# Residual and feed-forward products of 512 columns on split float32r operands

## Chip, cores and metric

One core of a Trainium2 chip runs the whole program. The metric is the device time in microseconds of one execution, as the median of the runs shown; lower is better.

## What is computed

Two hybrid layers (gated delta rule, latent attention and a gated recurrence, mixed by an output matrix) and then two layers of a second block: a feed-forward, a mixer, a second feed-forward. There are 256 tokens of width 1024, all in float32. What the change touches is this part of the reference (shortened):

```python
# hybrid layer, twice
return x + mixed @ w_out                     # mixed: 256 x 2048
...
# second block, l = 0, 1
x = x + 0.5 * swiglu(rms_norm(x, ffn1_norm[l]), ffn1_w_gate[l], ffn1_w_up[l], ffn1_w_down[l])   # width 2816
...
x = x + mixed @ w_out[l]                     # mixed: 256 x 1024
x = x + 0.5 * swiglu(rms_norm(x, ffn2_norm[l]), ffn2_w_gate[l], ffn2_w_up[l], ffn2_w_down[l])
```

## The kernel before, in words

Activations lie features first: a tile is 128 features by 256 tokens, and the residual `x` is eight such tiles. A product in float32 accuracy is made of three float32r products. Every operand is split into a high part and the rest (`split` for activations, `wsplit` for weights): ScalarE casts the high part (`h`, or `wh` for weights), VectorE subtracts it from the operand (`l`, or `wl`). `pair` gives the two parts of an activation as the two halves of one SBUF tile of 128 x 512. Then `mm3` (line 690) issues, per k tile of 128 features,

```python
mm(out, a[0], b[0], start=start, stop=False)   # wh, h
mm(out, a[0], b[1], start=False, stop=False)   # wh, l
mm(out, a[1], b[0], start=False, stop=stop)    # wl, h
```

with the weights stationary (128 x 128) and 256 tokens moving. `unit` (line 708) loops over the k tiles of 128 output features; all products of a unit go into one half of a PSUM bank. There are two rings of four banks, `acc` for such units and `mix` for everything else.

A feed-forward (`ffn`, line 819) has 22 hidden tiles. Per hidden tile a chunk of 1 MB of weights comes from DRAM (`raw`, three slots), gate and up are two units of 8 k tiles into the two halves of one `acc` bank, VectorE multiplies the bank by the norm's factor `rb` in one instruction of 512 columns, ScalarE takes the tanh, VectorE makes (tanh + 1) times gate and times up, and `split` makes the operand of the down product. Down runs over two groups of four output tiles with 22 k tiles each, in pieces of 6, 8 and 8. `feed` (line 808) adds a finished output tile to the residual, and for the next stage makes the split operand (`add_x`) and the sum of squares, which GpSimd accumulates. The output products of the hybrid layers (end of `hybrid`, units of 8 k tiles, twice over the eight tiles) and of the second block's mixers (`out_proj`, line 1587, units of 4 k tiles, twice over the eight tiles) end in `feed` too. In the second pass `feed` also makes the next stage's operand.

`wh` and `wl` have three slots of 128 x 1024 each, so a weight part is made when the unit three before it has ended.

The order of the instructions on each engine is set by a planner (`Order`): the kernel is traced first, each instruction gets a nominal cost (`cost`, line 378), and a list scheduling over the traced dependences writes one fixed order per engine. Each engine then runs its list in order. All instructions are issued at line 543, so rows of the trace are told apart by their tiles: `acc`, `mix`, `wh`, `wl`, `raw`, `x`, and `s` for the work tiles.

Of the kernel before, what the change touches and what calls it, by code (L numbers as in the profile page):

```python
# [13 lines left out]
ALU = mybir.AluOpType  # L14
# [3 lines left out]
P = 128  # L18
# [3 lines left out]
FF = 22  # hidden tiles of a feed-forward  # L22
# tile sizes (columns of 4 bytes) and their slots
SLOTS = {"raw": (2048, 3), "wh": (1024, 3), "wl": (1024, 3), "s1": (256, 20), "s2": (512, 48), "s3": (384, 12),
         "col": (24, 56)}
# order of the 64 rope dimensions: partners lie 16 lanes apart in a quadrant of 32
# [3 lines left out]
# ---------------------------------------------------------------- host layout  # L30
# [3 lines left out]
def _pack(W, chunks):  # L34
    """(first k tile, k tiles, columns) -> flat; each chunk lies [128, k tiles, columns]"""
    out = []
    for k0, kt, cols in chunks:
        w = W[k0 * P:(k0 + kt) * P][:, cols]
        out.append(w.reshape(kt, P, -1).transpose(1, 0, 2).reshape(-1))
    return np.concatenate(out)  # L40
# [46 lines left out]
# order of the 8 tiles of 128 that the second block's output products sum over: four that are ready early, then the rest  # L87
# [27 lines left out]
def gu_pack(G, U):  # L115
    w = np.stack([G.reshape(8, P, FF, P), U.reshape(8, P, FF, P)], axis=3)  # [k, p, j, 2, f]
# [7 lines left out]
# columns of the parameter tile: name -> (offset, columns)  # L124
# [17 lines left out]
def prm_pack(i):  # L142
# [6 lines left out]
    def taps(w):  # [4, C] -> [128, C/128 * 4]  # L149
# [34 lines left out]
# constants that depend on shapes alone  # L184
# [76 lines left out]
# ---------------------------------------------------------------- instruction order  # L261
# The kernel below is traced first; then each engine's instructions are put in an order that keeps the engines busy
# (a list scheduling over the traced dependences with the engines' nominal costs), and issued in that order.
ENG = ("tensor", "scalar", "vector", "gpsimd", "sync")
# how much later than the earliest of its ready instructions an engine may start a more urgent one
SLACK = {"tensor": 0.0, "scalar": 150.0, "vector": 40.0, "gpsimd": 100.0, "sync": 0.0}
PATIENCE = 400  # how far an instruction may fall behind its place in the tracing order
# free slots of a tag below which tiles are given out in tracing order only
RESERVE = {"s1": 6, "s2": 10, "s3": 4, "col": 16, "raw": 3, "wh": 3, "wl": 3, "mix": 2, "acc": 1}
# from the end of an instruction on one engine to the start of a dependent one on another  # L270
# [19 lines left out]
class Tracer:  # L290
    """stands for one engine: notes its instructions instead of issuing them"""
# [8 lines left out]
class Order:  # L300
# [10 lines left out]
    # ---- tracing  # L311
# [42 lines left out]
    def touch(self, op, r, w):  # L354
# [3 lines left out]
        if h is None:  # L358
            h = self.hist[name] = ([], [])  # writes, reads
# [18 lines left out]
    def cost(self, op):  # L378
# [7 lines left out]
        if op.eng == "tensor":  # L386
            rhs = a[2]
            m, n = _free(a[1]), _free(rhs) if fn == "matmul" else a[1].shape[0]
            if rhs.dtype == F32R:
                return max(0.833 * m, (n if n >= 256 else 4 * n) / 2.4) + 2.3, None  # L390
# [38 lines left out]
    # ---- scheduling  # L429
    def schedule(self):  # L430
        """each engine in turn takes, among the instructions that could start within its slack, the first traced; tiles
        get slots in tracing order, or past it while more than the tag's reserve is free"""
# [8 lines left out]
        # urgency: the tracing order for TensorE; for the others, the first TensorE instruction that needs the result  # L441
# [104 lines left out]
# ---------------------------------------------------------------- kernel  # L546
class Kern:
    def __init__(self, ctx, tc, aps):
# [20 lines left out]
        # scratch in DRAM: blocks of the delta rule's triangles, their inverses (zero outside the diagonal blocks)  # L569
# [6 lines left out]
    def start(self):  # L576
        """the first loads in the order of their use, and TensorE kept busy meanwhile, so that its clock is up"""
# [39 lines left out]
    # ---- tiles: few sizes, so that a slot serves every stage  # L617
# [31 lines left out]
    def pair(self):  # L649
        t = self.tile("s2", (P, 2, S), F32R)  # L650
        return t[:, 0, :], t[:, 1, :]
# [18 lines left out]
    # ---- weights: packed chunks streamed from DRAM in order, split exactly into two float32r parts  # L670
# [19 lines left out]
    def mm3(self, out, a, b, start, stop):  # L690
        """a: stationary parts, b: moving parts"""
# [1127 lines left out]
```

## Time and profile before

| | us |
|---|---|
| median of three runs | 1591.09 |
| lowest and highest run | 1589.70, 1593.88 |
| span of the profiled execution, first to last instruction | 1588.5 |
| lowest run less that span (what lies around it) | 1.2 |
| TensorE busy | 1569.5 |
| VectorE busy | 1183.2 |
| ScalarE busy | 836.4 |
| GpSimd busy | 191.8 |

The profile is of one execution. PE is TensorE's product, PEld its load of stationary weights, DVE is VectorE, ACT ScalarE, POOL GpSimd. A product's duration in a row holds the time in which others stream behind it, so cadences are read from the distance of starts. The granted clock is 1.00 at 2.4 GHz and 0.50 at 1.2 GHz.

### The profile page before, as it was taken

To read this page: it belongs to the slowest core of one execution; us is meant where nothing else is said; L and a number is where in the kernel's file an instruction comes from. 1 tells how busy PE (TensorE), PEld (TensorE's weight loads), DVE (VectorE), ACT (ScalarE), POOL (GpSimd) and SP (SyncE) were. 2 spreads that over 40 slices of the span, in tenths; PEclk is the share of its full clock that TensorE was granted. 3 is DMA by queue.
4 is the path that set the end of the run, shared out by engine and by line. 5 is a ranking of instruction groups with operands and counts; after the bars stand their busy time and mean duration, and the time that the engine had idled before them with its cause. 6 is when DMAs were issued, how large, how long until landed. Compare 5 with 4: busy or idle time off the path is not lost.

```text
span 1588.5 us, 31207 instructions
## 1 busy us (share of the span) xinstructions
PE 1569.5 (99%) x12712; PEld 1520.3 (96%) x12712; DVE 1183.2 (74%) x2249; ACT 836.4 (53%) x1508; POOL 191.8 (12%) x196
## 2 busy tenths in 40 slices
PE   8999999999999999999999999999999999999999
PEld 8988999988989999999999999999999998999999
DVE  8987968996987677756888777665777666777753
ACT  5467745547765544445445444555444456654442
POOL 2301002311114100002102000021000321110000
PEclk9999999999999999999999999999999999999999
DMA  8343445343435455454334555544555743355553
GB/s 283 118 140 107 171 140 179 119 143 107 163 133 186 160 186 184 175 185 147 123 117 159 186 186 173 185 176 162 184 186 175 244 145 107 121 173 186 179 173 126
DMA packets 54598, 257.82 MB, mean 162 GB/s; under 512 B 11308, under 2 KB 21688, under 8 KB 27576
## 3 DMA queue, kind: packets, MB, share of 16 engines
q1 hardware_dynamic: 54456, 255.85, 46.9%
q8 instruction: 99, 1.62, 0.4%
q14 instruction: 43, 0.35, 0.1%
HBM read 252.39 MB, written 3.43 MB: 161 GB/s over the span
## 4 chain that ended last, share of the span: by engine, by line
PE 85%; DVE 8%; POOL 2%; issue 2%; ACT 1%; DMA 1%; SPq 0%; POOLq 0%; DVEq 0%; ACTq 0%
PE acc L543 74%; PE mix L543 11%; DVE s L543 5%; DVE wl L543 2%; POOL col L543 1%; POOL s L543 1%; DVE col L543 1%; ACT s L543 1%; ACT wh L543 0%; DMA s<-tri_out 0%; DMA tri_out<-s 0%; DMA prm<-in_prm_dram 0%; SPq L543 0%; DVE x L543 0%; ACT L543 0%
## 5 line engine op out<-in xcount | busy, mean ns | idle before, releaser
L543 PE MATMUL acc<-s,wh 128*128 128x256 f32 x6720 | 1237.5, 285 | 0.0
L543 PEld LDWEIGHTS acc<-s,wh 128*128 128x128 f32 x6720 | 1051.8, 192 | 6.9 <-issue 4.6
L543 PE MATMUL acc<-s,wl 128*128 128x256 f32 x3360 | 957.1, 285 | 1.0 <-DVE wl L543 1.0
L543 ACT ACTIVATE wh<-raw 128x1024 fp32r<-128x1024 f32 (+1 forms) x470 | 489.1, 1041 | 574.9 <-PE acc L543 410.2
L543 DVE TENSOR_TENSOR wl<-raw,wh 128x1024 fp32r<-128x1024 f32 (+1 forms) x470 | 571.4, 1216 | 241.2 <-ACT wh L543 238.8
L543 PEld LDWEIGHTS acc<-s,wl 128*128 128x128 f32 x3360 | 644.9, 192 | 2.4 <-DVE wl L543 1.4
L543 PE MATMUL mix<-s,s 128*128 128x128 f32 (+7 forms) x1072 | 162.4, 291 | 5.7 <-DVE col L543 2.4
L543 POOL TENSOR_TENSOR s<-s,s 128x256 f32<-128x256 f32 x75 | 92.8, 1240 | 597.4 <-ACT s L543 596.2
L543 PEld LDWEIGHTS mix<-s,s 128*128 128x128 f32 (+5 forms) x1072 | 119.0, 168 | 34.8 <-issue 9.1
L543 ACT ACTIVATE s<-s 128x256 fp32r<-128x256 f32 (+3 forms) x311 | 134.1, 439 | 27.0 <-DVE s L543 25.3
L543 DVE TENSOR_TENSOR s<-s,s 128x256 fp32r<-128x256 f32 (+6 forms) x302 | 128.8, 436 | 13.5 <-ACT s L543 8.1
L543 PE MATMUL acc<-wh,s 128*128 128x256 f32 x640 | 126.5, 290 | 0.0
L543 DVE TENSOR_TENSOR s<-acc,s 128x512 f32<-128x512 f32 (+1 forms) x134 | 91.9, 686 | 44.2 <-PE acc L543 43.1
L543 PEld LDWEIGHTS acc<-wh,s 128*128 128x128 f32 x640 | 103.7, 194 | 2.3 <-issue 1.6
L543 PE MATMUL acc<-wl,s 128*128 128x256 f32 x320 | 92.5, 289 | 0.0
L543 ACT ACTIVATE s<-mix 32x64 f32<-32x64 f32 (+6 forms) x208 | 65.2, 327 | 50.2 <-PE mix L543 47.5
L543 DVE SCALAR_TENSOR_TENSOR s<-s,s 128x256 f32<-128x256 f32 (+2 forms) x168 | 81.8, 493 | 5.0 <-ACT s L543 4.8
L543 POOL TENSOR_TENSOR col<-col,mhalf 128x2 f32<-128x2 f32 (+2 forms) x31 | 44.7, 1442 | 228.8 <-DVE col L543 228.8
L543 POOL TENSOR_TENSOR s<-s,cst 128x256 f32<-128x256 f32 x36 | 33.6, 946 | 311.9 <-DMA s<-rows 161.3
L543 PEld LDWEIGHTS acc<-wl,s 128*128 128x128 f32 x320 | 62.1, 194 | 1.0 <-issue 1.0
L543 DVE SCALAR_TENSOR_TENSOR x<-acc,x 128x256 f32<-128x256 f32 x96 | 39.7, 419 | 29.2 <-PE acc L543 29.1
L543 PE MATMUL mix<-cst,s 128*128 128x128 f32 (+2 forms) x338 | 57.2, 267 | 3.7 <-DVE s L543 1.7
(94 smaller groups left out, 733.0 us busy)
## 6 DMA issues: line engine op xcount, KB each, us to landing
raw<-in_gu_dram SPq DMA_DIRECT2D x88, 1024.0 KB, 4.8
raw<-in_win_dram SPq DMA_DIRECT2D x36, 1024.0 KB, 5.0
raw<-in_dn_dram SPq DMA_DIRECT2D x32, 1024.0 KB, 4.8
raw<-in_wo_dram SPq DMA_DIRECT2D x24, 1024.0 KB, 4.8
raw<-in_wina_dram SPq DMA_DIRECT2D x13, 1024.0 KB, 4.8
raw<-in_dn_dram SPq DMA_DIRECT2D x16, 768.0 KB, 4.2
raw<-in_winb_dram SPq DMA_DIRECT2D x7, 1024.0 KB, 4.8
raw<-in_wkv_dram SPq DMA_DIRECT2D x6, 1024.0 KB, 4.8
```

The costliest lines, as they stand in the source:

```text
L543: getattr(getattr(self.nc, op.eng), op.fn)(*op.args, **op.kw)
```

## The change

In the feed-forwards and in the output products that end in the residual, one product of 512 columns with `wh` on both parts (`hl`) takes the place of two of 256; the product with `wl` is added to the upper half of the bank. So the sum lies in two halves, which are added later: in `feed` as two residual adds in a row, in gate and up by a copy of the upper half on ScalarE, an add on VectorE, and the multiplication by `rb` on GpSimd. Gate and up have a bank each. The planner's cost of a float32r product is another. Elsewhere (projections of the mixers) the three products stay. Comments are gone, and what only takes the third value of `pair` is left out here.

```diff
-                return max(0.833 * m, (n if n >= 256 else 4 * n) / 2.4) + 2.3, None
+                return max(0.9375 * m, (n if n >= 256 else 4 * n) / 2.4 + 2.5), None
...
     def pair(self):
         t = self.tile("s2", (P, 2, S), F32R)
-        return t[:, 0, :], t[:, 1, :]
+        return t[:, 0, :], t[:, 1, :], t
...
+    def unit_wide(self, ps, w, X, k0=0, first=True, last=True):
+        wh, wl = w
+        mm = self.nc.tensor.matmul
+        kt = wh.shape[1]
+        for k in range(kt):
+            h, _, hl = X[k0 + k]
+            mm(ps.rearrange("p (g t) -> p g t", g=2), wh[:, k, :], hl, start=first and k == 0, stop=False)
+            mm(ps[:, S:], wl[:, k, :], h, start=False, stop=last and k == kt - 1)
...
     def feed(self, j, ps, scale, stages):
-        nc.vector.scalar_tensor_tensor(x, ps, scale, x, ALU.mult, ALU.add)
+        for half in (ps[:, S:], ps[:, :S]):
+            nc.vector.scalar_tensor_tensor(x, half, scale, x, ALU.mult, ALU.add)
...
     def ffn(self, st, wgu, wdn, nxt):
...
-            ps = self.acc().rearrange("p (g t) -> p g t", g=2)
+            gs = self.s2()
             for g in range(2):
-                self.unit(ps[:, g, :], self.wsplit(raw[:, :, g * P:(g + 1) * P]), st["X"])
-            gs = self.s2()
-            nc.vector.tensor_tensor(gs, ps, st["rb"].unsqueeze(1).to_broadcast([P, 2, S]), ALU.mult)
+                ps = self.acc()
+                self.unit_wide(ps, self.wsplit(raw[:, :, g * P:(g + 1) * P]), st["X"])
+                low = self.s1()
+                nc.scalar.activation(low, ps[:, S:], AF.Copy)
+                nc.vector.tensor_tensor(gs[:, g, :], ps[:, :S], low, ALU.add)
+                nc.gpsimd.tensor_tensor(gs[:, g, :], gs[:, g, :], st["rb"], ALU.mult)
             th = self.s1()
             nc.scalar.activation(th, gs[:, 0, :], AF.Tanh, scale=0.5)
             nc.vector.scalar_tensor_tensor(th, th, 1.0, gs[:, 0, :], ALU.add, ALU.mult)
-            h = self.s1()
-            nc.vector.tensor_tensor(h, th, gs[:, 1, :], ALU.mult)
-            hs.append(self.split(h))
+            nc.vector.tensor_tensor(th, th, gs[:, 1, :], ALU.mult)
+            hs.append(self.split(th))
...
-                self.unit(pss[j][:, :S], self.wsplit(raw[:, :, jj * P:(jj + 1) * P]), hs, k0, k0 == 0, k0 + kt == FF)
+                self.unit_wide(pss[j], self.wsplit(raw[:, :, jj * P:(jj + 1) * P]), hs, k0, k0 == 0, k0 + kt == FF)
...
-                    self.feed(4 * g + j, pss[j][:, :S], 0.25, nxt)
+                    self.feed(4 * g + j, pss[j], 0.25, nxt)
...
-                    self.unit(ps[:, :S], self.wsplit(raw[:, :, jj * P:(jj + 1) * P]), M, 8 * kk)
-                    self.feed(2 * c + jj, ps[:, :S], 1.0, nxt if kk == 1 else [])
+                    self.unit_wide(ps, self.wsplit(raw[:, :, jj * P:(jj + 1) * P]), M, 8 * kk)
+                    self.feed(2 * c + jj, ps, 1.0, nxt if kk == 1 else [])
...
-                        self.unit(ps[:, :S], (wh[:, :, f], wl[:, :, f]), M, 4 * kk)
-                        self.feed(4 * c + jj + i, ps[:, :S], 1.0, nxt if kk else [])
+                        self.unit_wide(ps, (wh[:, :, f], wl[:, :, f]), M, 4 * kk)
+                        self.feed(4 * c + jj + i, ps, 1.0, nxt if kk else [])
```

What the planner's lists hold now, at the places that the prediction speaks of. In the rows a tile's name ends in its number, and the words ahead of the arrow are what is written. First VectorE in the first feed-forward's gate/up, one hidden tile; before (`acc_1556` is the bank of gate and up together):

```order
L543 TENSOR_TENSOR s_1482_1561<-acc_1556,s_1357_1436 128x512
L543 TENSOR_TENSOR wl_1578<-raw_1575,wh_1577 128x1024
L543 SCALAR_TENSOR_TENSOR s_1483_1562<-s_1483_1562,s_1482_1561 128x256
L543 TENSOR_TENSOR s_1484_1563<-s_1483_1562,s_1482_1561 128x256
L543 TENSOR_TENSOR wl_1580<-raw_1575,wh_1579 128x1024
L543 TENSOR_TENSOR s_1485_1564<-s_1484_1563,s_1485_1564 128x256
```

and in the change (`acc_1577` is gate, `acc_1581` up, `s_1497` the scaled gate and up, `s_1506` the tanh, `s_1507` the split operand):

```order
L543 TENSOR_TENSOR s_1497_1576<-acc_1577,s_1501_1580 128x256
L543 TENSOR_TENSOR wl_1603<-raw_1599,wh_1602 128x1024
L543 TENSOR_TENSOR s_1497_1576<-acc_1581,s_1505_1584 128x256
L543 SCALAR_TENSOR_TENSOR s_1506_1585<-s_1506_1585,s_1497_1576 128x256
L543 TENSOR_TENSOR s_1506_1585<-s_1506_1585,s_1497_1576 128x256
L543 TENSOR_TENSOR wl_1607<-raw_1599,wh_1606 128x1024
L543 TENSOR_TENSOR s_1507_1586<-s_1506_1585,s_1507_1586 128x256
```

The multiplication by `rb` has left VectorE's list, and two adds of 256 columns, one on each side of a `wl`, stand where it was.

ScalarE in the same stage, in the change (`acc_1557` and `acc_1565` are the up of one hidden tile and the gate of the next):

```order
L543 ACTIVATE wh_1578<-raw_1575 128x1024
L543 ACTIVATE s_1481_1560<-acc_1557 128x256
L543 ACTIVATE s_1482_1561<-s_1473_1552 128x256
L543 ACTIVATE wh_1582<-raw_1575 128x1024
L543 ACTIVATE s_1489_1568<-acc_1565 128x256
L543 ACTIVATE s_1483_1562<-s_1482_1561 128x256
```

A copy out of PSUM now stands behind each cast of weights, and the tanh (third row) stands ahead of the next cast.

TensorE in the same stage, in the change (`s_1299`, `s_1305` and so on are the eight k tiles of the operand, here with both parts):

```order
L543 MATMUL acc_1565<-s_1299_1378,wh_1566 128x512
L543 MATMUL acc_1565<-s_1299_1378,wl_1567 128x256
L543 MATMUL acc_1565<-s_1305_1384,wh_1566 128x512
L543 MATMUL acc_1565<-s_1305_1384,wl_1567 128x256
L543 MATMUL acc_1565<-s_1312_1391,wh_1566 128x512
L543 MATMUL acc_1565<-s_1312_1391,wl_1567 128x256
```

Where three products of 256 columns stood for a k tile, one of 512 and one of 256 stand now; the whole list has 2496 rows of 128x512.

## Rows read from the trace of the kernel before

**Rows 1.** The page: part 1, engines; part 4, chain by engine.

```profile
PE 1569.5 (99%) x12712; PEld 1520.3 (96%) x12712; DVE 1183.2 (74%) x2249; ACT 836.4 (53%) x1508; POOL 191.8 (12%) x196
...
PE 85%; DVE 8%; POOL 2%; issue 2%; ACT 1%; DMA 1%; SPq 0%; POOLq 0%; DVEq 0%; ACTq 0%
```

**Rows 2.** Groups by shape: count, busy us, mean ns, idle before.

```profile
L543 PE MATMUL acc<-s,wh 128*128 128x256 f32 x6720 | 1237.5, 285 | 0.0
```

**Rows 3.** Timeline of PE in gate/up: start us, duration us, instruction, count.

```profile
900.08 0.28 PE L543 MATMUL acc<-s,wl 128*128 128x256 f32 x1
900.20 0.40 PE L543 MATMUL acc<-s,wh 128*128 128x256 f32 x2
900.44 0.28 PE L543 MATMUL acc<-s,wl 128*128 128x256 f32 x1
```

**Rows 4.** Timeline of PE, 12 stationary columns.

```profile
1096.46 2.92 PE L543 MATMUL acc<-s,s 128*12 128x256 f32 x24
1099.22 0.40 PE L543 MATMUL acc<-s,wh 128*128 128x256 f32 x2
```

**Rows 5.** Timeline of PE, plain f32 products.

```profile
747.20 1.89 PE L543 MATMUL mix<-s,s 128*128 128x256 f32 x8
748.93 0.38 PE L543 MATMUL mix<-cst,s 128*128 128x128 f32 x2
```

**Rows 6.** Stretches: length, busy (count) of PE, PEld, DVE, ACT, POOL; clock; DMA.

```profile
870.00:996.00 126.00, 125.99 (x1050) 126.00 (x1051) 92.58 (x135) 59.72 (x88) 0.71 (x1) 1.00 0.52 179
997.00:1060.00 63.00, 63.00 (x527) 63.00 (x526) 39.84 (x49) 33.45 (x50) 8.20 (x7) 1.00 0.54 188
```

**Rows 7.** Groups by shape, ScalarE and VectorE.

```profile
L543 ACT ACTIVATE wh<-raw 128x1024 fp32r<-128x1024 f32 x430 | 455.2, 1059 | 528.2 <-PE acc L543 383.0 <-issue 134.6 <-ACT s L543 9.9
...
L543 ACT ACTIVATE s<-s 128x256 f32<-128x256 f32 x120 | 47.4, 403 | 1.6 <-DVE s L543 0.7 <-DMA s<-in_mem_dram 0.5
...
L543 DVE SCALAR_TENSOR_TENSOR x<-acc,x 128x256 f32<-128x256 f32 x96 | 39.7, 419 | 29.2 <-PE acc L543 29.1
...
L543 ACT ACTIVATE s<-acc 128x256 f32<-128x256 f32 x32 | 11.8, 380 | 10.6 <-PE acc L543 9.2 <-DVE s L543 0.6
```

**Rows 8.** Timeline of VectorE in gate/up; idle time ahead in brackets.

```profile
900.36 1.23 DVE L543 TENSOR_TENSOR wl<-raw,wh 128x1024 fp32r<-128x1024 f32 x1 [0.87 <-ACT wh L543]
901.50 0.42 DVE L543 TENSOR_TENSOR s<-s,s 128x256 fp32r<-128x256 f32 x1
902.20 0.69 DVE L543 TENSOR_TENSOR s<-acc,s 128x512 f32<-128x512 f32 x1 [0.29 <-PE acc L543]
903.22 1.22 DVE L543 TENSOR_TENSOR wl<-raw,wh 128x1024 fp32r<-128x1024 f32 x1 [0.33 <-ACT wh L543]
904.37 0.42 DVE L543 SCALAR_TENSOR_TENSOR s<-s,s 128x256 f32<-128x256 f32 x1
```

**Rows 9.** Timeline of VectorE and GpSimd, end of the first hybrid layer; GpSimd alone.

```profile
254.99 1.23 DVE L543 TENSOR_TENSOR wl<-raw,wh 128x1024 fp32r<-128x1024 f32 x1 [0.43 <-ACT wh L543]
256.13 0.96 DVE L543 SCALAR_TENSOR_TENSOR s<-x,prm,s 128x256 fp32r<-128x256 f32 x1
...
255.41 1.41 POOL L543 TENSOR_TENSOR s<-s,s 128x256 f32<-128x256 f32 x1 [1.46 <-ACT s L543]
...
298.07 0.73 POOL L543 TENSOR_TENSOR s<-s,cst 128x256 f32<-128x256 f32 x1 [1.51 <-DVE s L543]
```

**Rows 10.** Timeline of VectorE and PE, end of an output projection.

```profile
859.55 0.42 DVE L543 SCALAR_TENSOR_TENSOR x<-acc,x 128x256 f32<-128x256 f32 x1
859.88 0.63 DVE L543 SCALAR_TENSOR_TENSOR s<-x,prm,s 128x256 fp32r<-128x256 f32 x1
...
868.20 1.75 DVE L543 TENSOR_TENSOR wl<-raw,wh 128x1024 fp32r<-128x1024 f32 x1
869.88 0.47 DVE L543 SCALAR_TENSOR_TENSOR s<-x,prm,s 128x256 fp32r<-128x256 f32 x1
...
870.01 0.38 PE L543 MATMUL acc<-s,wl 128*128 128x256 f32 x1 [0.48 <-DVE wl L543]
```

More of the change, by code (lines that the diff above doesn't have):

```diff
@@ L698, in split @@
         nc = self.nc
-        h, l = self.pair()
+        h, l, hl = self.pair()
         if scale is None:
@@ L705, in split @@
             nc.vector.scalar_tensor_tensor(l, src, scale, h.bitcast(F32), ALU.mult, ALU.subtract)
-        return h, l
+        return h, l, hl
     def unit(self, out, w, X, k0=0, first=True, last=True):
@@ L756, in bcast @@
         nc = self.nc
-        h, l = self.pair()
+        h, l, _ = self.pair()
         for b in range(2):
@@ L970, in gdn_rows @@
             gh = [gd[:, b, 2 * hp + h:2 * hp + h + 1] for b in range(2)]
-            lh, ll = self.pair()
+            lh, ll, _ = self.pair()
             V.tensor_scalar(lh[:, :P], gt, gh[0], None, ALU.mult)
```

## The prediction

> **What bounds the kernel now.** I read the page's busy shares and its chain first. TensorE (PE) is busy for 1569.5 of 1588.5 us, and the chain that ended last is 85% PE, 8% VectorE (DVE) [rows 1]. So time is won where PE gets shorter, and lost where another engine makes PE wait. Next, the groups by shape: the 128x256 products on `wh` alone are 6720 instructions [rows 2]. Their mean of 285 ns is pipelined and is no cadence. The cadence is read from PE's timeline inside a gate/up stage: from one `wl` product at 900.08 to the next at 900.44 lie three products in 360 ns, so 120 ns each [rows 3]. At 2.4 GHz 256 columns are 107 ns, and the granted clock there is 1.00 [rows 6], so about 13 ns of each product are not columns.
>
> Two rows say what those 13 ns are. The 24 products with only 12 stationary columns, again 256 moving columns, take 1099.22 - 1096.46 = 2.76 us, 115 ns each [rows 4]: smaller weights, shorter cadence, so the load is part of the 120. And eight plain f32 products of 128x256, each with a full 128x128 load, take 1.73 us, 216 ns each [rows 5]: twice the column time (213 ns) and almost nothing on top. Under a long product a full load is hidden.
>
> The stage table shows PE full everywhere it matters: 126 of 126 us in gate/up, with VectorE at 92.6 and ScalarE (ACT) at 59.7, while GpSimd (POOL) has 0.7; in down VectorE has 39.8 of 63 [rows 6].
>
> **Part 1, two products in place of three.** Per k tile the change has one 512-column product with `wh` and one 256-column product with `wl`. The columns stay 768; one load and one start go. The count is 1408 k tiles in gate/up (4 feed-forwards x 22 hidden tiles x 16), 704 in down (4 x 8 x 22), 256 in the hybrid layers' output (2 x 16 x 8) and 128 in the other two output projections (2 x 16 x 4): 2496 in all. The trace has no 512-column product of this type. Bounds: 213 ns, its columns alone, with 115 for the short one as in rows 4, is 328 per k tile and saves 32; 240, twice the 120, saves nothing. I take 216 as in rows 5, the nearest row (same streaming time, same load under it), plus 120 for the short product, which has to cover the next load: 336 ns, 24 less than 360. 2496 x 24 = **59.9 us less**, 33.8 of it in gate/up.
>
> The Trainium skill weighs against this part: "TensorE: Matmul & The Clock Gate", section "Back-to-back issue gap", gives an isolated product N/2.4 + 2.5 ns, so by it joining two products would save 2.5 ns per k tile, an estimate of 6 us in all. The 120 ns of rows 3 are not its 109, so the trace does not agree for 256 columns.
>
> **Part 2, gate and up.** Before, one VectorE product of 0.69 us per hidden tile read the bank that gate and up shared [rows 8]. Now gate and up have a bank each, and of each ScalarE copies 256 columns out of PSUM (0.38 us), VectorE adds the other 256, and GpSimd multiplies [rows 7]. The add reads one PSUM operand, as the residual's add does, which takes 0.42 us. ScalarE gets 2 x 0.38 = 0.76 us more on 59.7 x 5.76 / 126 = 2.7 us per hidden tile [rows 6], and stays far below 5.38. No DMA changes. A bank is freed two instructions later than before, and the four `acc` banks now hold four units of 2.69 us instead of four hidden tiles; three units are 8 us, against about 4 us that I reckon from the end of a unit to its add.
>
> GpSimd's 176 multiplies are the hard part. Alone such an instruction takes 0.73 us; beside VectorE it took 1.41, waiting for the 1.23 us `wl` subtraction, and the next VectorE instruction with two SBUF operands then took 0.96 [rows 9] where 0.47 is usual [rows 10]. The two take turns at something. A VectorE instruction that reads PSUM takes 0.42 either way.
>
> So I walk VectorE's queue for one hidden tile, in the order shown (add gate, `wl`, add up, tanh+1, times up, `wl`, split). The next start lies 1.14 us behind that of a `wl`, 0.33 behind that of a short one (901.50 - 900.36 [rows 8] and 859.88 - 859.55 [rows 10]). From the end of add gate: `wl` to 1.14; the gate multiply has waited for it and ends 0.60 later, at 1.74 (256.82 - 256.22 in rows 9); the add of up runs beside it; the multiply of up follows, to 2.48. Meanwhile the tanh (0.40 [rows 7]) ends at 2.2, and the tanh+1 product, blocked by GpSimd as the split in rows 9, ends 0.27 behind it at 2.75. Times up ends at 3.2. ScalarE's cast for the next `wl` is queued behind the tanh (2.2 + 1.06 [rows 7]), so with a hand-over of 0.1 `wl` starts at 3.4 and ends at 4.6; split 4.9, next add 5.3. A round of **5.3 us, against PE's 16 x 0.336 = 5.38**. VectorE just keeps up, with none of the 1.5 us idle per tile that rows 8 show now (0.87 + 0.29 + 0.33). If GpSimd gets its turn before the first `wl`, the same walk gives 5.5. I put 0.05 us per hidden tile, 88 x 0.05 = **4 us back**; bounds 0 and 88 x 0.12 = 11.
>
> **Part 3, residual adds.** Each of 96 adds becomes two in a chain, 96 x 0.33 = 32 us of VectorE, most of it in idle time. Not in the short output projections: a unit is 4 k tiles, 1.34 us now. Their last eight units already fill VectorE, and PE waits there 0.48 us for a `wl` that took 1.75 [rows 10]. Eight more adds are 2.7 us, PE arrives 8 x 0.1 = 0.8 us sooner, and the earlier eight units leave some backlog: about 4 us of waiting, twice, 8 us. In the hybrid layers an add, the wait for the cast (0.43), `wl` and the blocked split fill one unit of 8 x 0.36 = 2.88 us [rows 9]; the second add goes into that wait, and the round is about 2.79 against 2.69: 0.8 us over eight units. At the end of each stage the next one waits for the last residual tile, 0.5 us later with the extra add and its latency. So two hybrid ends at 1.3, three feed-forward ends at 0.9 (four such units in a row), the kernel's end 0.4: 5.7 us. Together **14 us back**; bounds 4, where only the ends count, and 25.
>
> **Sum.** 1588.5 - 59.9 + 4 + 14 = 1546.6 us of span. The median of the runs is 2.6 us above the span; so **1549 us**. The planner also gets another cost for these products, so other stages are ordered a little differently; I price that at nothing, give or take 4 us, by the PE gaps of a fraction of a microsecond that such places show now (0.48 in rows 10).
>
> **Rivals.** (a) *Half the saving.* If the 13 ns are paid once per product, however long it is, the 512-column product takes 227 and a k tile 347: 33 us less, and 1588.5 - 33 + 14 + 2.6 = 1572. For it: 115 ns with hardly any weights is still 8 above the columns. Against: rows 5, where the surplus is 3.
>
> (b) *Columns alone cost.* The 512-column product takes 240: nothing is saved, the residual adds stay, 1588.5 + 12 + 2.6 = 1603. For it: an exact 120 in every product. Against: rows 4 and 5. The rule of the Trainium skill's "TensorE: Matmul & The Clock Gate" quoted above goes in this direction and gives an estimate near 1597.
>
> (c) *GpSimd's turns make VectorE the bound in gate/up.* Nothing overlaps: 0.42 + 0.90 for the multiply + 1.22 + 0.42 + 0.42 + 0.80 + 0.42 + 1.22 + 0.42 = 6.24 us per hidden tile. Then 88 x (6.24 - 5.38) = 76 us come back: 1588.5 - 59.9 + 14 + 76 + 2.6 = 1621, slower. It decides from 5.90 us per hidden tile (no gain) and 5.95 (measurably slower). For it: rows 9, where both engines were held. Against: the walk, in which the add of up runs beside a multiply, and GpSimd's wait lies behind a `wl` that must run anyway. On such turns the Trainium skill's "SBUF — State Buffer", section "Who interferes with whom", says that a VectorE instruction with two SBUF inputs and a GpSimd one that reads SBUF exclude each other for the whole instruction; by that rule (c) is what happens wherever the next VectorE instruction is of this kind.
>
> That one 512-column product is in truth issued as two is excluded by the order, which has 2496 rows of 128x512.
>
> **How the numbers follow.** Forecast 0.74, with a range of its own of 1532 to 1572 (18 to 28 ns per k tile, 8 to 28 us back); (a) 0.12 at 1572; (b) 0.07 at 1603; (c) 0.07 at 1621. The range of **1530 to 1584** takes in the forecast and (a) with a late drain, and leaves out (b) and (c) and some of the tails. A measurement here can tell about 0.3%, 4.8 us. Faster: forecast and (a), 0.86. Within 0.3%: the edge of (b), where the long product takes 3 ns less than 240, and of (c) between 5.85 and 5.95 us, 0.05. Slower: the rest, 0.09.
>
> **What would show it.** Part 1: a k tile of 336 ns in PE's timeline in the down stages, where VectorE has room; 347 means (a), 360 (b). Part 2: gate/up stages of 22 x 5.4 = 119 us with PE idle for `wl` or a bank only now and then; 6 us per hidden tile and VectorE over 95% busy there mean (c). Part 3: PE waiting on VectorE at the ends of the output projections, about 4 us each. PE's idle time over the whole span should rise by some 15 to 20 us. I am wrong if the k tile is not between 330 and 347, or if the waits in gate/up pass 20 us in all.

## The result and the profile after

The changed kernel takes **1604.85 us** (median of 5 runs, 1601.81 to 1609.28) against 1591.09 before (5 runs, two more than in the table above, 1588.27 to 1593.88): a ratio of 1.0092, 95% interval [1.0068, 1.0116]. It is slower, by three times what a measurement can tell, and lies 21 us above the predicted range.

The changed kernel's page, part 1 (busy us, share of the span, instructions) and part 4 (chain by engine), answers to [rows 1]:

```profile
PE 1566.0 (98%) x10216; PEld 1397.9 (87%) x10216; DVE 1206.1 (75%) x2433; ACT 890.7 (56%) x1684; POOL 338.3 (21%) x372
...
PE 48%; DVE 2%; POOL 1%; ACT 1%; issue 1%; POOLq 0%; ACTq 0%; DVEq 0%
```

The shares of the chain add up to 53% only, since it is followed back no further than 758 us; nothing is read from it here. PE issues 2496 products fewer, as counted, but is busy only 3.5 us less, and the span is 1601.7. So its idle time has grown from 1588.5 - 1569.5 = 19.0 to 35.7 us. That is 16.7 more idle and 3.5 less busy: 13.2 us.

Span and mean granted clock, of the kernel before and then of the changed one:

```profile
core 0: 1588.5 us, clock 0.991
```

```profile
core 0: 1601.7 us, clock 0.980
```

The clock has two levels, so a mean of 0.980 is 2 x 0.020 x 1601.7 = 64 us at 1.2 GHz, against 29 before. Time at half clock loses half its work, so PE's busy time holds some 18 us that come from the clock. Without them the products themselves had become 21 us shorter. Both losses, waits and clock, have to be placed.

The stretches of the two hybrid layers (us; length, then busy of PE, PEld, DVE, ACT, POOL, with counts; PE's clock; DMA share; GB/s), before:

```profile
0.00:260.30 260.30, 253.36 (x1977) 236.01 (x1978) 218.46 (x524) 151.97 (x312) 43.72 (x59) 0.99 0.49 165
260.30:513.30 253.00, 250.88 (x1962) 234.26 (x1961) 212.15 (x481) 155.09 (x324) 49.48 (x46) 0.97 0.41 138
```

and the same stages of the changed kernel:

```profile
0.00:265.70 265.70, 255.44 (x1856) 231.65 (x1857) 221.72 (x541) 153.61 (x312) 45.02 (x59) 0.98 0.48 162
265.70:531.00 265.30, 258.54 (x1835) 233.81 (x1834) 218.17 (x497) 154.22 (x323) 52.62 (x46) 0.94 0.39 132
```

This is the surprise: the hybrid layers, in which only the output product has changed, are 5.4 and 12.3 us longer, 17.7 together. All the rest, with 2240 of the 2496 shortened k tiles, is only 4.5 us shorter. In those two layers PE is idle for 8.0 us more than before (17.0 against 9.1) and busy for 9.7 us more, with fewer products. PE's waits in the first 531 us of either trace (us in total, times, longest; before, this takes in 18 us of the next stage), before:

```profile
PE mix L543 <- POOL s L543: 2.6, 5, 1.1
PE acc L543 <- DVE s L543: 2.2, 2, 1.5
...
PE mix L543 <- DVE s L543: 0.9, 3, 0.4
PE acc L543 <- ACT s L543: 0.6, 1, 0.6
```

and in the changed kernel:

```profile
PE mix L543 <- DVE s L543: 4.5, 6, 1.5
PE mix L543 <- POOL s L543: 3.4, 5, 1.4
PE acc L543 <- ACT s L543: 2.9, 3, 1.8
PE acc L543 <- DVE s L543: 2.8, 3, 1.3
```

They are many small waits, most of them of mixer products for their producers. One of them, a unit `acc<-wh,s` that the change does not touch, on PE's timeline before (start, duration, and idle time ahead in brackets):

```profile
436.69 0.28 PE L543 MATMUL acc<-s,wl 128*128 128x256 f32 x1
436.81 0.28 PE L543 MATMUL acc<-wh,s 128*128 128x256 f32 x1
436.94 0.28 PE L543 MATMUL acc<-wl,s 128*128 128x256 f32 x1
```

and in the changed kernel:

```profile
449.97 0.28 PE L543 MATMUL acc<-s,wl 128*128 128x256 f32 x1
452.00 0.39 PE L543 MATMUL acc<-wh,s 128*128 128x256 f32 x1 [1.75 <-ACT s L543]
...
453.63 0.58 PE L543 MATMUL acc<-wh,s 128*128 128x256 f32 x1 [0.64 <-DVE s L543]
454.00 0.42 PE L543 MATMUL acc<-wl,s 128*128 128x256 f32 x1
454.22 0.63 PE L543 MATMUL acc<-wh,s 128*128 128x256 f32 x2
```

Before, the unit followed without a gap. Now PE reaches it 1.75 us too early, waits again 0.64, and behind the second wait the products run at half speed (0.22 us from the start at 454.00 to the next at 454.22, where 436.81 to 436.94 is 0.13). So this wait is paid twice: itself, and a stretch at half clock behind it, 13.7 us from 453.5 on.

Not every wait is paid so. The changed kernel's trace has some 45 waits of PE and nine stretches at half clock, the longest of 20.5 us. And the kernel before has a stretch at half clock near this place too, 6.8 us from 441.4 on, behind a wait of 0.84 us:

```profile
439.66 5.43 PE L543 MATMUL mix<-s,s 64*128 64x128 f32 x14 [0.84 <-POOL s L543]
...
446.46 0.41 PE L543 MATMUL acc<-s,wl 128*128 128x256 f32 x1
...
447.10 0.41 PE L543 MATMUL acc<-s,wl 128*128 128x256 f32 x1
```

There three products take 0.64 us, where they take 0.36 at full clock. What has grown is the sum, 63 us at half clock against 27 by the clock's records.

The k tile itself, on PE's timeline of the changed kernel in gate/up of the second block's first feed-forward and of its later one, answers to [rows 3]:

```profile
599.70 0.40 PE L543 MATMUL acc<-s,wh 128*128 128x512 f32 x1
599.94 0.28 PE L543 MATMUL acc<-s,wl 128*128 128x256 f32 x1
600.06 0.40 PE L543 MATMUL acc<-s,wh 128*128 128x512 f32 x1
...
600.76 0.40 PE L543 MATMUL acc<-s,wh 128*128 128x512 f32 x1
...
1200.24 0.39 PE L543 MATMUL acc<-s,wh 128*128 128x512 f32 x1
...
1200.58 0.39 PE L543 MATMUL acc<-s,wh 128*128 128x512 f32 x1
...
1200.93 0.39 PE L543 MATMUL acc<-s,wh 128*128 128x512 f32 x1
```

Three k tiles take 1.06 us in the first place (599.70 to 600.76), 353.3 ns each; the later ones take 347 (1200.24 to 1200.58 to 1200.93). Over the whole trace a k tile keeps one of these two rates for a stage at a time: 346.7 in the hybrid layers' outputs and the feed-forward from 1118 us on (784 k tiles), 353.3 in the other 1712. Neither is the 336 of the forecast.

### The profile page after: what moved, and what is told of

It reads as the page before. It is cut to its first block, busy times and chain, and to the rows that moved or that the text cites. A ratio compares the mean times of both kernels' runs of the same rounds, so it can differ in the third digit from the quotient of the medians.

```text
span 1601.7 us, 27064 instructions
## 1 busy us (share of the span) xinstructions
PE 1566.0 (98%) x10216; PEld 1397.9 (87%) x10216; DVE 1206.1 (75%) x2433; ACT 890.7 (56%) x1684; POOL 338.3 (21%) x372
## 4 chain that ended last, share of the span: by engine, by line
PE 48%; DVE 2%; POOL 1%; ACT 1%; issue 1%; POOLq 0%; ACTq 0%; DVEq 0%
PE acc L543 44%; PE mix L543 4%; POOL col L543 1%; DVE s L543 1%; POOL s L543 0%; ACT s L543 0%; DVE col L543 0%; ACT wh L543 0%; DVE x L543 0%; DVE wl L543 0%; POOLq L543 0%; ACTq L543 0%; DVEq L543 0%
## 5 line engine op out<-in xcount | busy, mean ns | idle before, releaser
L543 PE MATMUL acc<-s,wh 128*128 128x512 f32 (+1 forms) x4224 | 1218.9, 354 | 1.6 <-DVE x L543 1.6
L543 PEld LDWEIGHTS acc<-s,wh 128*128 128x128 f32 x4224 | 745.2, 191 | 118.4 <-issue 3.9
L543 POOL TENSOR_TENSOR s<-s,s 128x256 f32<-128x256 f32 x251 | 224.2, 895 | 729.8 <-ACT s L543 356.5
L543 PE MATMUL mix<-s,s 128*128 128x128 f32 (+7 forms) x1072 | 168.4, 302 | 7.6 <-DVE col L543 2.9
L543 ACT ACTIVATE s<-s 128x256 f32<-128x256 f32 (+3 forms) x311 | 135.0, 444 | 37.6 <-DVE s L543 35.7
L543 DVE TENSOR_TENSOR s<-s,s 128x256 f32<-128x256 f32 (+6 forms) x302 | 130.0, 443 | 33.3 <-POOL s L543 30.4
L543 DVE TENSOR_TENSOR s<-acc,s 128x256 f32<-128x256 f32 (+2 forms) x222 | 104.2, 470 | 9.0 <-PE acc L543 8.1
L543 ACT ACTIVATE s<-acc 128x256 f32<-128x256 f32 (+2 forms) x231 | 88.6, 386 | 29.4 <-PE acc L543 25.4
L543 DVE SCALAR_TENSOR_TENSOR x<-acc,x 128x256 f32<-128x256 f32 x192 | 78.1, 419 | 26.4 <-PE acc L543 23.7
L543 POOL TENSOR_TENSOR s<-s,cst 128x256 f32<-128x256 f32 x36 | 46.5, 1305 | 161.6 <-DVE s L543 72.4
```

What stands on the lines that cost most here:

```text
L543: getattr(getattr(self.nc, op.eng), op.fn)(*op.args, **op.kw)
```

## The experiments

Theory A: the planner's new cost for products (120 ns instead of 109 for 256 columns) changes the order in the mixer stages for the worse. Theory B: the work added to ScalarE, VectorE and GpSimd makes PE wait. All ratios are to the kernel before, on the same chip.

### One part at a time

```diff
-                return max(0.9375 * m, (n if n >= 256 else 4 * n) / 2.4 + 2.5), None
+                return max(0.833 * m, (n if n >= 256 else 4 * n) / 2.4) + 2.3, None
```

The changed kernel with this line as before (e1):

> The changed kernel with the old nominal cost of a float32r product in the planner; all products and instructions as in the change. In the changed kernel the two hybrid layers, whose own products are all but the same, end 17.7 us later than before (last residual add at 530.6 against 512.9 us). Theory A (the new cost gives a worse order in the mixer stages): those stages go back to where they were before, about 19 us come back, 1584 to 1589 us. Theory B (the added copies, adds and multiplies make TensorE wait): the order of the hybrid layers does not matter, 1602 to 1608 us.

The kernel before with the new line and nothing else, so the same diff reversed (e2):

> The kernel before with nothing but the new nominal cost in the planner. Theory A: slower by the same 15 to 20 us, 1606 to 1611 us, with the loss in the two hybrid layers. Theory B: within 3 us of the kernel before, 1588 to 1594 us.

The old line, wide products into the residual alone, `ffn`'s gate and up with `self.unit(ps[:, g, :], ...)` as before (e3):

> Old cost; the 512-column products only where they end in the residual (down and the output projections, 1088 k tiles), gate and up as before. From the changed kernel's k tile of 346 to 354 ns I expect 6 to 14 ns saved per k tile, 7 to 15 us, and about 5 us lost at the ends of stages. Theory A: 1580 to 1589 us. Theory B: the second residual add is the loss, above 1595 us.

The old line, wide products in gate and up alone, `feed` with one add as before (e4):

> Old cost; the 512-column products only in gate and up (1408 k tiles), with the copy, add and multiply; the residual as before. Theory A: 9 to 18 us saved and little lost, 1574 to 1584 us. Theory B: the copy, add and multiply are the loss, above 1595 us.

| run | median us | ratio, interval |
|---|---|---|
| e1, all wide, old cost | 1581.79 | 0.9943 [0.9924, 0.9962] |
| e2, kernel before, new cost | 1619.67 | 1.0174 [1.0148, 1.0200] |
| e3, residual wide, old cost | 1591.49 | 1.0004 [0.9986, 1.0022] |
| e4, gate and up wide, old cost | 1580.43 | 0.9934 [0.9911, 0.9956] |

Theory A holds. The cost line alone makes the kernel before 28 us slower; taken out of the changed kernel it gives 23 us back, and the hybrid layers then take 262.8 and 253.4 us. Two sizes came out otherwise than expected: e2 lost more than 15 to 20 us, and e3 lies between its two ranges. The new line brings PE's waits for VectorE's `s` into the kernel before as well; in the first 531 us of e2, where the kernel before had 0.9 us of them:

```profile
PE mix L543 <- DVE s L543: 5.2, 5, 1.5
```

The wide products by themselves are worth some 10 us, all of it gate and up; the residual's are worth nothing as the order stands.

### Why a truer cost gives a worse order

The new cost is the truer one: 120 ns is just what a 256-column product takes [rows 3] (a 512-column product is planned at 216 ns by either line). But by the planner's formulas the weights' low part (`wl`) costs 1135 ns and is 1239 in the trace of the kernel before; a cast of weights costs 946 and is 1059, and a 256-column ScalarE instruction out of SBUF 306 and is 403 [rows 7]. So the new line has slowed PE alone in the plan.

More time between a producer's end and the PE instruction that needs it; the changed kernel with its new cost (e5):

```diff
-       "scalar": {"tensor": 285.0, "vector": 143.0, "gpsimd": 180.0, "sync": 100.0},
+       "scalar": {"tensor": 685.0, "vector": 143.0, "gpsimd": 180.0, "sync": 100.0},
...
```

(vector 270 to 670 and gpsimd 290 to 690 likewise)

> The changed kernel with its new cost line, and 400 ns more between the end of a ScalarE, VectorE or GpSimd instruction and the earliest start that the planner gives to a TensorE instruction that needs it. Theory A1 (with the dearer products the planner puts TensorE's mixer products so close behind their producers that on the chip they come first and wait): the margin gives the waits back; about 1582 us (1574 to 1592), the two hybrid layers together near 516 us instead of 531, half-clock time near 30 us instead of 65. Rival A2 (the new order is worse for another reason, such as which tiles hold the slots): the margin changes nothing of it, 1598 to 1612 us.

Or ScalarE's and VectorE's planned durations 8% longer, in all their formulas but those of memset and reciprocal (e6):

```diff
-            return d, table
+            return 1.08 * d, table
...
-        return d + 1.042 * n, None
+        return 1.08 * (d + 1.042 * n), None
```

> The changed kernel with its new cost line, and ScalarE's and VectorE's planned durations raised by 8%, so that they are nearer to what the trace shows (the weights' low part takes 1.225 us, planned 1.135). A1 (it is the ratio of TensorE's planned speed to the producers' that counts, and the old cost had it right by two errors that cancel): about 1582 us (1574 to 1592), as in the run with the old cost. A2: 1598 to 1612 us, as the changed kernel.

The 400 ns of e5 in e4 (e7):

> The old cost line, 512-column products in gate and up alone, and the same 400 ns more ahead of TensorE. A1: what waits are left in the mixer stages shrink too; 1565 to 1580 us against 1580 without the margin. A2, or a margin that makes products late that could have run: 1578 to 1600 us.

Both edits in the changed kernel (e9):

> The changed kernel with its new cost line, ScalarE's and VectorE's planned durations raised by 8%, and 400 ns more ahead of TensorE. A3 (what counts first is the ratio of the planned speeds, because an engine planned too fast falls ever further behind its plan; a margin helps once the ratio is right): the 20 us that the margin gave with the old cost come here too, 1556 to 1570 us. A4 (the margin's gain belongs to the old cost line, or to a kernel whose residual products are short): 1576 to 1592 us, no better than with the 8% alone.

The 400 ns in the kernel before (e11):

> The kernel before, with nothing but 400 ns more ahead of TensorE. A3: the margin is worth as much without wide products, 1566 to 1578 us against 1591. A4: 1584 to 1596 us.

| run | median us | ratio, interval |
|---|---|---|
| e5, changed kernel, 400 ns | 1598.96 | 1.0054 [1.0030, 1.0078] |
| e6, changed kernel, others 8% longer | 1580.34 | 0.9930 [0.9905, 0.9954] |
| e9, changed kernel, both | 1564.12 | 0.9816 [0.9759, 0.9873] |
| e7, gate and up wide, old cost, 400 ns | 1559.87 | 0.9806 [0.9784, 0.9829] |
| e11, kernel before, 400 ns | 1577.64 | 0.9912 [0.9880, 0.9945] |

A1 as first put failed for the margin: with 400 ns (e5) the time lies outside A1's range and just inside that of its rival A2, and the 6 us that it gave back are hardly clear of noise (its interval overlaps the changed kernel's, 1.0068 to 1.0116). With the new cost kept, longer planned durations of the other two engines gave all of it back (e6), as A1 has it and A2 does not. And with the old cost, or with the new one and the 8%, the margin is worth 14 to 21 us on top: e11 against the kernel before, e9 against e6, e7 against e4. That is what A3 forecast (e11 at the upper end of its range; e7 had come out 5 us below the one put for it), and A4 is out. PE's waits in the first 531 us of e6, for the rows of the changed kernel above:

```profile
PE acc L543 <- DVE s L543: 2.1, 4, 0.8
...
PE mix L543 <- POOL s L543: 1.6, 3, 1.0
...
PE mix L543 <- DVE s L543: 0.4, 2, 0.2
```

and of e7:

```profile
PE acc L543 <- DVE s L543: 2.2, 2, 1.4
PE mix L543 <- POOL s L543: 1.4, 2, 0.9
...
PE mix L543 <- DVE s L543: 0.7, 2, 0.4
```

The mixer products' wait for VectorE's `s` falls from 4.5 us to 0.4 and 0.7. That engines planned too fast fall further and further behind their plan is the reading that fits e5 and e6, but it is argued and not shown: which instruction first falls behind was not followed, and a single factor, 8%, was tried. That the orders of e6 and e9 are better for another reason, as A2 has it, or by chance, is not excluded. What is shown is that the planner's costs alone, with every instruction kept, move the time by 23 to 28 us (e1, e2, e6). The stage times of single profiles are no proof by themselves: with the old cost the first hybrid layer took 260 us in e4 and 270 to 271 in e3 and e8, where more of it ran at half clock.

### What a product costs

Two k tiles at a time in e4 (e8), and in e7 (e10):

```diff
-        for k in range(kt):
-            h, _, hl = X[k0 + k]
-            mm(ps.rearrange("p (g t) -> p g t", g=2), wh[:, k, :], hl, start=first and k == 0, stop=False)
-            mm(ps[:, S:], wl[:, k, :], h, start=False, stop=last and k == kt - 1)
+        for k in range(0, kt, 2):
+            for n in (k, k + 1):
+                mm(ps.rearrange("p (g t) -> p g t", g=2), wh[:, n, :], X[k0 + n][2], start=first and n == 0, stop=False)
+            for n in (k, k + 1):
+                mm(ps[:, S:], wl[:, n, :], X[k0 + n][0], start=False, stop=last and n == kt - 1)
```

> The old cost line, 512-column products in gate and up alone, two k tiles at a time: both 512-column products, then both 256-column ones. Theory C1 (a product costs its columns and 13 ns once, and the 7 ns more in some stages come from a product of 512 columns that follows one of 256, whose own loading has only 120 ns to hide in): a pair of k tiles takes 693 to 700 ns in every stage, 1571 to 1577 us. Rival C2 (the 7 ns come with a rhythm that a stage falls into at its start, whatever the order): 707 ns in some stages and 693 in others, 1576 to 1584 us.

> The old cost line, 512-column products in gate and up alone, two k tiles at a time, and 400 ns more ahead of TensorE. If the order of the two products and the margin are separate causes, their gains add up: 1559.9 less what the pairs still save in the stages that ran at 353 ns a k tile, 1550 to 1558 us. If the pairs' 10 us came from a better order by chance: 1558 to 1570 us.

e8 took 1570.78 us (0.9894 [0.9845, 0.9943]), e10 1559.32 (0.9793 [0.9746, 0.9841]). PE's timeline of e10 in gate/up (two products in a row):

```profile
600.09 0.63 PE L543 MATMUL acc<-s,wh 128*128 128x512 f32 x2
600.56 0.39 PE L543 MATMUL acc<-s,wl 128*128 128x256 f32 x2
600.79 0.62 PE L543 MATMUL acc<-s,wh 128*128 128x512 f32 x2
```

A pair takes 0.70 us (600.09 to 600.79); over the trace 697 ns, 348.4 per k tile, in all four feed-forwards of e8 and of e10. So in pairs the slower rate is gone, as C1 forecast. C1's reason, the short product ahead of a long one, cannot be all of it, since products in turn ran at 346.7 too. In e4 the gate/up stages ran at 353.3 almost throughout, so pairs save 1408 x 4.9 = 7 of the 10 us there (the intervals of e4 and e8 overlap). In e7 three of four ran at about 347 already: by the rates pairs save 1.7 us in the fourth and cost about as much in the three, and e10 gained nothing. Its expected 1550 to 1558 was missed, and by its time alone it lies in the range put for a better order by chance. What puts a stage on one rate or the other stays open; it is not the code, since the second feed-forward of one kernel ran at 346.8 in one trace and at 353.3 in another (e13 and e17 below).

The surplus over the columns, measured at a third length: e7 with 384 columns (e18). Left out are the low part's products for tokens 128 to 255; the low-weight product goes to the first half.

```diff
-            mm(ps.rearrange("p (g t) -> p g t", g=2), wh[:, k, :], hl, start=first and k == 0, stop=False)
-            mm(ps[:, S:], wl[:, k, :], h, start=False, stop=last and k == kt - 1)
+            mm(ps[:, :384], wh[:, k, :], hl.rearrange("p g t -> p (g t)")[:, :384], start=first and k == 0, stop=False)
+            mm(ps[:, :S], wl[:, k, :], h, start=False, stop=last and k == kt - 1)
```

> The first of these three with 384 columns in place of 512 in the long products of gate and up; the low part's products for tokens 128 to 255 are left out, and the low-weight product goes into the first half. G1 (about 13 ns once per product, whatever its columns): the long product takes 173 ns (160 and 13), a k tile 293, or 300 in a stage of the slower rhythm; 1408 x 53 = 75 us less than the full width, about 1485 us. G2 (the surplus grows with the columns, 240 in 512 and so 180 in 384): a k tile of 300 ns everywhere, about 1494 us. G3 (2.5 ns a product, and the 120 of a 256-column product come from the load of its weights): 163 and a k tile of 283 ns, about 1470 us.

It took 1506.84 us in its one run. PE's timeline in its gate/up:

```profile
573.48 0.34 PE L543 MATMUL acc<-s,wh 128*128 128x384 f32 x1
573.65 0.28 PE L543 MATMUL acc<-s,wl 128*128 128x256 f32 x1
573.77 0.34 PE L543 MATMUL acc<-s,wh 128*128 128x384 f32 x1
```

A k tile takes 0.29 us (573.48 to 573.77); its median over the trace is 293 ns, G1 to the nanosecond. The columns of 256, 384 and 512 take 107, 160 and 213 ns at full clock, so a k tile of three short products holds 40 ns besides its columns, and one of two 26 with 384 columns and 27 with 512 (at 346.7): about 13 for each product, whatever its length. That is a mean over the k tile: from start to start the long product has some 16 on top (176 ns, and 230 at 512) and the short one behind it 10 (117). The total is 22 us above G1's all the same, because VectorE now sets the pace in most of each gate/up stage; its timeline there:

```profile
574.09 1.23 DVE L543 TENSOR_TENSOR wl<-raw,wh 128x1024 fp32r<-128x1024 f32 x1 [0.49 <-ACT wh L543]
...
577.04 0.96 DVE L543 TENSOR_TENSOR s<-s,s 128x256 fp32r<-128x256 f32 x1
...
579.15 1.23 DVE L543 TENSOR_TENSOR wl<-raw,wh 128x1024 fp32r<-128x1024 f32 x1 [0.48 <-ACT wh L543]
```

A hidden tile takes 5.06 us there (574.09 to 579.15) where 16 k tiles of 293 ns are 4.69, and the split, 0.42 in the changed kernel (below), takes 0.96.

### What the residual's products are worth

The changed kernel with the old cost and 400 ns (e12):

> The changed kernel with the old cost line and 400 ns more ahead of TensorE; against the run with gate and up alone (1559.9 us) it shows what the residual's 512-column products and second adds are worth where TensorE seldom waits. D1 (the residual products save 7 to 13 ns on some 1,060 k tiles and give it back in part at the ends of output projections): 1550 to 1558 us. D2 (they save nothing, since the second add of each tile is late for the next stage): 1558 to 1568 us.

1562.75 us (1559.78 to 1566.11), 0.9816 [0.9766, 0.9866]: D2 by its time. The two stages that end in an output projection take 2.5 and 4.1 us more in its trace than in e7's. PE's timeline of e12 at the second of them:

```profile
1354.94 0.50 PE L543 MATMUL acc<-s,wh 128*128 128x512 f32 x1 [0.66 <-DVE x L543]
...
1355.81 0.63 PE L543 MATMUL acc<-s,wh 128*128 128x512 f32 x1
...
1356.45 0.63 PE L543 MATMUL acc<-s,wh 128*128 128x512 f32 x1
```

PE waits 0.66 us until a residual add has emptied a bank, and the k tiles behind it take 640 ns (1355.81 to 1356.45): half clock again, and just the 768 columns at 1.2 GHz. So the output projections go back to three products and one add (e13), then with pairs everywhere (e14), and then with 800 ns (e15):

```diff
-                        self.unit_wide(ps, (wh[:, :, f], wl[:, :, f]), M, 4 * kk)
-                        self.feed(4 * c + jj + i, ps, 1.0, nxt if kk else [])
+                        self.unit(ps[:, :S], (wh[:, :, f], wl[:, :, f]), M, 4 * kk)
+                        self.feed(4 * c + jj + i, ps[:, :S], 1.0, nxt if kk else [])
```

(`feed` adds twice for a tile of 512 columns and once for one of 256)

> As the run with the old cost line, everything wide and 400 ns ahead of TensorE (1562.75 us), but the output projections of the two middle mixers, whose sums close after four k tiles, again with three products and one add. R1 (there the second add leaves PSUM full, TensorE waits for VectorE about 0.7 us at a time and its clock halves; that stage cost 138.5 instead of 136.0 us and the other 105.3 instead of 101.2): 1555 to 1559 us. R2 (those waits are noise of one profile, and what the residual part loses lies at the starts of the next stages): 1560 to 1566 us.

> The same with two k tiles at a time in all 512-column products. R3 (348.4 ns a k tile in every stage, where 346.7 and 353.3 alternate by stage now): within 4 us of the run without pairs on either side, and with less spread. R4 (a k tile's time has nothing to do with the stages' total while TensorE waits elsewhere): the same to 0.1%, and half-clock stretches unchanged.

> The same again with 800 ns instead of 400 ahead of TensorE. If waits in the mixer stages are still what is left: 2 to 8 us less. If 400 ns had taken nearly all of them, or products now come later than they could: the same or up to 8 us more.

Then e7 and e13 once more, side by side (e16 and e17):

> The run with the old cost line, gate and up alone and 400 ns (1559.9 us) once more, on the same chip as the next one. R1: 5 to 10 us slower than the next one. R2, or a difference between chips: within 3 us of it.

> The run with gate, up, down and the hybrid layers' output wide, the output projections not (1552.6 us), once more. R1: 1549 to 1556 us and 5 to 10 below the one before. R2: within 3 us of it.

| run | median us | lowest, highest | ratio, interval |
|---|---|---|---|
| e13, output projections narrow | 1552.60 | 1548.42, 1553.99 | 0.9752 [0.9726, 0.9778] |
| e14, the same in pairs | 1553.62 | 1552.70, 1555.49 | 0.9767 [0.9740, 0.9795] |
| e15, in pairs, 800 ns | 1558.57 | 1549.93, 1563.75 | 0.9790 [0.9759, 0.9821] |
| e16, gate and up alone | 1558.94 | 1558.34, 1561.03 | 0.9823 [0.9802, 0.9843] |
| e17, as e13 | 1551.87 | 1551.37, 1553.22 | 0.9774 [0.9754, 0.9794] |

R1 holds: without the two output projections the residual part gains 7 us (e17 against e16, no run of one reaching the other), and with them it gains nothing that can be told (e12 against e7, ratios 0.9816 and 0.9806). From e12 to e13 the gain was larger than R1 had it, 10 us for 4 to 8. In the two traces it is 10.8 us, and only 4.5 of them lie in the two stages that end in an output projection (138.5 to 135.4 and 105.3 to 103.9 us). Another 6 to 7 come from the second and third feed-forward, whose k tiles ran at 353 ns in e12 and at 347 in e13; in e17, the same kernel as e13, the second ran at 353 again. So about half of the 10 us is R1's, and the rest of that gain is a matter of the rate. Pairs change nothing here (R3). 800 ns bring nothing over 400, with more spread. The kernel of e13 and e17, at 1552 us, is the fastest: it beats the kernel before by 2.3 to 2.5% and the changed kernel by 53 us.

## Why the prediction was wrong

**"I price that at nothing, give or take 4 us"**, of the planner's new cost, is the step that turned the sign. It was worth 23 us in the changed kernel (e1) and 28 in the kernel before (e2). The price was taken from the size of PE's gaps, but a cost changes where every mixer product stands, not how long one gap is; and with the waits came 35 us more at half clock, which no term held. No rival held it either. How the new cost makes the order worse is argued only, as said above.

**Part 1, "I take 216 as in rows 5"**, is the mis-sized term. The long product takes 230 to 236 ns from start to start, the short one behind it 117, and the k tile 346.7 or 353.3. So the saving by cadence is 784 x 13.3 + 1712 x 6.7 = 22 us instead of 59.9. Rival (a) named the mechanism, 13 ns once per product and 347 ns, and e18 bears it out at a third length; the slower rate of 353.3 came on top. The nearest row was the wrong one: plain f32 products stream as long, but theirs is a surplus of 3 ns [rows 5], and the 13 of the split type did not shrink under a longer product. So "Under a long product a full load is hidden" did not carry over, and what the 13 ns are stays open. The rule of the Trainium skill's "TensorE: Matmul & The Clock Gate", "Back-to-back issue gap", 2.5 ns a product, would have given 6 us by the prediction's estimate; the k tiles measured saved 6.7 to 13.3 ns each, so the trace agrees with neither it nor the forecast.

**Part 2, "4 us back", bounds 0 and 11,** held. VectorE's timeline in gate/up of the changed kernel, one hidden tile:

```profile
1205.28 1.22 DVE L543 TENSOR_TENSOR wl<-raw,wh 128x1024 fp32r<-128x1024 f32 x1 [0.79 <-ACT wh L543]
1206.42 0.42 DVE L543 TENSOR_TENSOR s<-acc,s 128x256 f32<-128x256 f32 x1
...
1207.80 0.42 DVE L543 TENSOR_TENSOR s<-s,s 128x256 f32<-128x256 f32 x1 [0.63 <-POOL s L543]
1208.15 1.22 DVE L543 TENSOR_TENSOR wl<-raw,wh 128x1024 fp32r<-128x1024 f32 x1
1209.28 0.42 DVE L543 TENSOR_TENSOR s<-s,s 128x256 fp32r<-128x256 f32 x1
...
1210.83 1.23 DVE L543 TENSOR_TENSOR wl<-raw,wh 128x1024 fp32r<-128x1024 f32 x1 [0.79 <-ACT wh L543]
```

The round is 1210.83 - 1205.28 = 5.55 us, and 16 x 0.3467 is 5.55: PE sets it. The time agrees: gate and up alone (e4) saved 10 to 11 us, and its 1408 k tiles at 353.3 ns save 9.4, so nothing was given back there. VectorE still idles 0.79 + 0.63 us in it, and the multiplies find room where the walk had VectorE stand still. Rival (c) is out for this kernel, though e18 shows it close: with a k tile of 293 ns VectorE's round is the bound.

**Part 3, "14 us back", of it 8 in the output projections.** The place was right and the size too large. PE's waits for residual adds, of which the kernel before has none, all lie in the two output projections of the changed kernel:

```profile
PE acc L543 <- DVE x L543: 1.6, 2, 1.0
```

The wait of rows 10 was misread: it lies in the feed-forward behind the output projection and not in its last eight units, since both the `wl` (868.20) and the product (870.01) start after the last residual add, at 866.91. It fell from 0.48 us to 0.18 in the changed kernel, and PE waits there for the sum of squares instead, 1.06 us at either output projection. With these, PE waits about 3 us more than before at the two output projections, for the 8 put there, and about 1.3 more at the other five stage starts, for 5.7 with the kernel's end. By its time e3 gives back about 8 us in all, give or take 3: its k tiles save that much, and it came out as the kernel before. That is inside the bounds of 4 and 25. Taking the wide form out of the output projections gained about 4.5 us in their own stages (e12 to e13).

**The sum, corrected:** 38 us less saved and 23 lost to the order would make 1549 into 1610; 1604.85 was measured, so by subtraction parts 2 and 3 gave back some 5 us less than the 18 put there. By e3 and e4 it was about 10 less, so some 5 us have no place. "PE's idle time should rise by some 15 to 20 us" came true, 16.7, but little more than 4 us of it are part 3's waits, and 8.0 are the mixers' waits in the two hybrid layers: a right number for a wrong reason, and so luck.

## What to carry to other kernels

Where a planner sets the order, a change of one cost is a change of every stage: test it alone, in the old code, before the work that it comes with. Costs that are all short in about the same proportion gave a better order here than one true cost among short ones, and some margin ahead of the bounding engine was worth nearly as much as the wide products themselves (14 us alone, and 18 for gate and up with it). Here a longer matmul saved the fixed part of the ones it replaced and no more, so read that part from products of the same type; and keep it out of units so short that the extra work on their results cannot be hidden.

## What the runs showed of the hardware

- A float32r product cost its columns at 2.4 GHz and about 13 ns, on the mean of a k tile, with 256, 384 and 512 columns alike: 360 ns for three of 256, 293 for one of 384 and one of 256 (e18), 346.7 for one of 512 and one of 256.
- At half clock that surplus did not show: 768 columns took 640 ns, as one product of 512 and one of 256 (e12, 1355.81 to 1356.45) and as three of 256 (the kernel before, 446.46 to 447.10).
- With 512- and 256-column products in turn a k tile ran at one of two rates, 346.7 or 353.3 ns, for a stage at a time and with the same code (the second feed-forward of e13 and of e17); in pairs it was 348.4 in every feed-forward of e8 and e10.
- Some waits of PE had products at half clock behind them: the clock fell at 453.5 us of the changed kernel, behind waits of 1.75 and 0.64 us, and at 1355.7 us of e12, behind one of 0.66. Most waits had none. The profiled runs with right ratios and 400 ns of margin had a mean granted clock of 0.991 to 0.997, the changed kernel 0.980.
